# Second mixer: two more gates ahead of the transposes of branch B's keys, and fill products between the latents' steps

## The chip, the cores and the metric

The kernel runs on one core of a Trainium2 chip. The metric is the device time of one execution in microseconds (us), lower is better. One core has a matrix engine (TensorE, PE in the rows, with its weight loads as PEld), a vector engine (VectorE, DVE), an activation engine (ScalarE, ACT), a general one (GpSimd, POOL), and a queue that issues the DMAs (SyncE, SP). They run side by side and wait for each other through semaphores.

## The reference

A backbone of two layers over 256 latent tokens and 256 context tokens, 1024 wide. Each layer: a SwiGLU half step, three token mixers on one normalised input, a gated merge with an output projection, and a second SwiGLU half step. The context is an un-noised prefix; only the latent stream is returned.

```python
D_MODEL = 1024; SEQ = 256; CTX_LEN = 256; DEPTH = 2; D_FF = 2816
A_HEADS = B_HEADS = C_HEADS = 8; A_KV_HEADS = B_KV_HEADS = 2; HEAD_DIM = 64
C_NOPE_DIM, C_ROPE_DIM, C_V_DIM, C_Q_RANK, C_KV_RANK = 64, 32, 64, 384, 256
...
def mla_keys_values(c_kv, k_rope, p, rope):
    kv = heads(rms_norm(c_kv, p["c_kv_lat_norm"]) @ p["c_w_ukv"], C_HEADS)
    k_nope, v = kv[..., :C_NOPE_DIM], kv[..., C_NOPE_DIM:]
    k_rope = jnp.broadcast_to(k_rope[:, :, None, :], k_nope.shape[:-1] + (C_ROPE_DIM,))
    k = rms_norm(jnp.concatenate([k_nope, k_rope], axis=-1), p["c_k_norm"])
    return rope_tail(k, C_ROPE_DIM, rope), v
```

In words: A is grouped-query attention over a window with a sink, B the same over everything with normalised, rotated queries and keys, C attends through low-rank latents for queries and for keys and values. Each branch's output is projected, multiplied by a sigmoid gate of the normalised input (1024 columns for each branch), and the three are summed and projected.

## The kernel before, in words

**Products.** Everything is float32, and each product is made of three matmuls of rounded operands, high by high, high by low and low by high (`mm3`, L101 to L103). `split` makes the two halves of an operand: ScalarE copies the high one (L108), VectorE subtracts it (L109).

**Weights.** They come in chunks. `fetch` issues the DMA of a chunk on SP's queue (L172) into one of two `raw` buffers (q4 buffers alternate with them from the end of the mixer on, see below) and its split into `whi` and `wlo`, of which there are eight each. Chunks are fetched two ahead of their use. A chunk's DMA waits until the buffer's last chunk has been split, and the splits stand in the queues of ScalarE and VectorE among everything else these engines do.

**Order.** PE runs its instructions in the order of the program. The other engines' queues are laid out by a scheduler, which decides what stands ahead of what there.

**The mixer** (`mixer`, L1012). PE does attention in steps, and each step leaves PE with something to wait for: the scores of 128 queries against 512 keys (S, L710), a softmax on VectorE, ScalarE (exponential, L727) and GpSimd (scaling by the reciprocal sum, `p`, L736), four transposes of the result (T, L754), a split of them into `pth` and `ptl`, and after every second step a weighted sum of the values (O, L762 and L763). The scores have two PSUM buffers, so S of a step needs the exponential of two steps before. T stands two or three steps behind its S. Branch A has 16 steps, B 16 and C 16 (S0 to S15, two for each head).

Between these, `fill` draws on a list of products that nothing in the attention waits for: gates (24 matmuls of 128x256 each in the second mixer), branch B's queries (`w_bq`), the merges of finished branches (`w_br`), and the latents that branch C needs (`w_cq`, `w_ckv`). A generator runs through them in one order; `FILLS[l]` says how many us of it are drawn where in mixer `l`:

- `keys` and `start`: before and after the transposes of branch A's keys; `q`: ahead of the first scores of A; `a` and `b`: in each step of A and B
- `latent`: between the steps of `latent_heads` (L861: transposes of the normalised latents, L867); `ups`: before the products with `w_uq` and `w_ukv` that make C's queries and keys; `c0`: before C's attention; `c`: in each step of C
- at the end `fill(1e3)` draws all that is left

Inside the generator (L1073 to L1100) stand also the steps that prepare branch B: `prep_k` normalises and rotates B's keys (VectorE and GpSimd, L618 to L630; the last of it are the two multiplications by the gain, L630), and `k_heads` transposes them on PE (L670, four transposes, one for each 128 tokens, from the buffers `vh`, `vh`, `vh` and `th`).

At the end of the mixer `begin` (L186) copies a value of the last head's keys into `start`; from then on every second chunk goes to a q4 buffer, whose DMA waits for a copy from `start` on GpSimd (L154). The q4 buffers, three of them, hold C's keys until then. Then comes the merge of branch C (eight times 12 matmuls), which needs the whole output of C.

The second mixer does only the latent tokens (`last`), so its gates have 256 columns.

Of the kernel before, what the change touches and what calls it, by code (L numbers as in the profile page):

```python
# [14 lines left out]
KD = 8  # L15
# [12 lines left out]

FILLS = (
    dict(a=2.0, b=1.7, keys=0.0, start=9.0, q=3.0, latent=2.0, ups=5.0, c0=9.0, c=2.5),  # L30
    dict(a=2.0, b=1.8, keys=3.0, start=10.0, q=3.0, latent=0.0, ups=2.0, c0=0.0, c=1.3),
)
ADA_LOOK = 3
DEPTH_AB, DEPTH_C = 3, (2, 3)
# [24 lines left out]
class Kernel:  # L59
# [952 lines left out]
    def mixer(self, l, last, after):  # L1012
# [52 lines left out]
        def fill():  # L1065
            def gates(ds):
                for d in ds:
                    m.append(self.T(f"x{d}", [128, NT]))
                    yield from self.gate_tanh(l, 0, d, whole, m[d][:, whole])

            yield from gates(range(1))
            self.prep_k(g3, 1)
            yield from gates(range(1, 4))  # L1073
            self.K[1] = self.k_heads(g3, 1)
            self.rope_tables64((G_BQ,))
            bq.extend(self.raw4(512))
            yield from self.tok_product(l, "w_bq", 512, 2, bq, qtts, "d")
            left = list(qtts)
            for i, us in enumerate(gates(range(4, KD))):
                if left and i % 3 == 0:  # L1080
                    tt = left.pop(0)
                    self.prep_heads(bq[tt].rearrange("p (h d) -> p h d", h=8), G_BQ, tt, 8, self.rq[1][:, tt])
                yield us
            early = []
            if last:

                early += [v[:, HALF[1]] for v in m]
                for d in range(KD):
                    yield from self.gate_tanh(l, 1, d, whole, early[d])
            yield from self.merge(l, 0, y[0], m, whole, lambda: self.at > na)  # L1090
            c = self.T("m0", [128, 4, 384])
            cq.extend(c[:, tt] for tt in range(4))
            yield from self.tok_product(l, "w_cq", 384, 2, cq, qtts, "d")
            self.latent_norm(l, cq, 384, G_CQL, qtts)
            have.append(True)
            c = self.T("m1", [128, 4, 288])
            ckv.extend(c[:, tt] for tt in range(4))
            yield from self.tok_product(l, "w_ckv", 288, 3, ckv, (0, 1, 2, 3), "d")
            self.latent_norm(l, ckv, 256, G_CKVL, range(4))
            have.append(True)  # L1100
            yield from self.merge(l, 1, y[1], m, whole, lambda: ready, early)
            for i in (3, 4):
                c = self.T(f"m{i}", [128, 4, NT])
                ths.extend(c[:, j] for j in range(4))
            for d in range(KD):
                yield from self.gate_tanh(l, 2, d, whole, ths[d][:, whole])

        us = FILLS[l]
        fill = self.filler(fill())
        self.K = [None, None]  # L1110
        fill(us["keys"])
        self.K[0] = self.k_heads(g3, 0)
        fill(us["start"] - us["keys"])
        self.attention(steps, preps, lambda: fill(us["a"] if self.at < na else us["b"]), depth, lambda: fill(us["q"]))
        t3 = [self.T("q4", [128, 2, NT], F32R, bufs=Q4) for _ in range(3)]
# [11 lines left out]
        q = self.T("m6", [128, 4, 8, 96])  # L1127
# [32 lines left out]
        for d in range(0, KD, 2):  # L1160
            c = self.T(("pth", "ptl")[d // 2 % 2], [128, 2, NT], bufs=2)
# [4 lines left out]
        for v, tag, n, bufs in ((out[0], "m0" if last else "m5", 4, 1), (out[1], "m6", 6, 1), (out[1], "q4", 2, Q4)):  # L1166
            c = self.T(tag, [128, n, NT], F32R, bufs=bufs)
# [214 lines left out]
```

## Time and profile before

| | |
|---|---|
| Time, three runs | 2151.74, 2152.40 and 2154.44 us, median 2152.4 |
| The profiled execution | 2153.58 us, its span 2151.8 us |
| PE busy | 2097.2 us, 97% of the span |
| Chain of waits: PE, DVE | 90%, 5% |
| Granted TensorE clock, mean | 0.993 |
| Second mixer | about 1640 to 1926 us of the span |

The span runs from the first to the last instruction. The granted clock is a share of 2.4 GHz: 1.00 means that level, 0.50 means 1.2 GHz, and values between are means over a stretch with both. In a row of the timeline stand the start, the duration, engine, line, operation, output and inputs by the program's names, shape, how many such instructions the row takes together, and in brackets the idle time of the engine ahead of it and what ended it. Matmuls are pipelined: their durations overlap, and the pitch is read from the distance of two starts.

### The profile page before, as it was taken

To read this page: it belongs to the slowest core of one execution; us is meant where nothing else is said; L and a number is where in the kernel's file an instruction comes from. 1 tells how busy PE (TensorE), PEld (TensorE's weight loads), DVE (VectorE), ACT (ScalarE), POOL (GpSimd) and SP (SyncE) were. 2 spreads that over 40 slices of the span, in tenths; PEclk is the share of its full clock that TensorE was granted. 3 is DMA by queue.
4 is the path that set the end of the run, shared out by engine and by line. 5 is a ranking of instruction groups with operands and counts; after the bars stand their busy time and mean duration, and the time that the engine had idled before them with its cause. 6 is when DMAs were issued, how large, how long until landed. Compare 5 with 4: busy or idle time off the path is not lost.

```text
span 2151.8 us, 33450 instructions
## 1 busy us (share of the span) xinstructions
PE 2097.2 (97%) x11832; PEld 1829.3 (85%) x11832; DVE 1526.0 (71%) x3121; ACT 1008.5 (47%) x2026; POOL 445.1 (21%) x854
## 2 busy tenths in 40 slices
PE   6999999999999999999999999999999799999999
PEld 3888888888898888988888898888888798899999
DVE  5587777779888766658665666856568888986665
ACT  4323233567675664432323343232336676665554
POOL 3121110444234220202010031201105412511000
PEclk9999999999999999999999999999999899999999
DMA  8565555321113224256444326555543332345663
GB/s 297 194 203 176 175 174 167 98 79 53 45 49 104 68 64 143 79 182 199 149 153 140 107 82 204 191 173 181 175 145 110 109 99 76 104 142 177 188 187 120
DMA packets 95527, 299.17 MB, mean 139 GB/s; under 512 B 10880, under 2 KB 15616, under 8 KB 94976
## 3 DMA queue, kind: packets, MB, share of 16 engines
q1 hardware_dynamic: 95360, 297.04, 43.0%
q8 instruction: 93, 1.52, 0.3%
q14 instruction: 74, 0.61, 0.1%
HBM read 292.80 MB, written 4.19 MB: 138 GB/s over the span
## 4 chain that ended last, share of the span: by engine, by line
PE 90%; DVE 5%; ACT 1%; POOL 1%; DMA 1%; issue 1%; SPq 0%; POOLq 0%; ACTq 0%; DVEq 0%
PE pd L101 13%; PE pd L102 13%; PE pd L103 13%; PE ps L101 7%; PE ps L103 7%; PE ps L102 7%; PE pv L101 7%; PE pv L103 7%; PE pv L102 7%; PE ps L710 3%; PE pt L754 2%; PE pv L763 1%; DVE wlo L109 1%; PE pv L762 1%; POOL w L408 1%
## 5 line engine op out<-in xcount | busy, mean ns | idle before, releaser
L108 ACT ACTIVATE whi<-raw 128x512 fp32r<-128x512 f32 (+2 forms) x521 | 314.8, 611 | 466.9 <-PE pd L102 141.2
L109 DVE TENSOR_TENSOR wlo<-raw,whi 128x512 fp32r<-128x512 f32 (+2 forms) x521 | 349.9, 677 | 163.5 <-ACT whi L108 159.7
L108 ACT ACTIVATE whi<-q 128x512 fp32r<-128x512 f32 (+1 forms) x299 | 184.3, 620 | 380.2 <-PE pd L102 102.3
L101 PE MATMUL pd<-hh,whi 128*128 128x512 f32 (+1 forms) x864 | 304.5, 352 | 3.1 <-ACT hh L409 1.9
L102 PE MATMUL pd<-hl,whi 128*128 128x512 f32 (+1 forms) x864 | 302.1, 350 | 1.2 <-DVE hl L410 1.1
L103 PE MATMUL pd<-hh,wlo 128*128 128x512 f32 (+1 forms) x864 | 301.5, 349 | 0.0
L109 DVE TENSOR_TENSOR wlo<-q,whi 128x512 fp32r<-128x512 f32 (+1 forms) x299 | 200.4, 674 | 121.2 <-ACT whi L108 119.6
L154 POOL COPY q<-start 1x1 f32<-1x1 f32 x151 | 54.5, 362 | 656.2 <-DVE wlo L109 472.6
L101 PEld LDWEIGHTS pd<-hh,whi 128*128 128x128 f32 x864 | 163.8, 190 | 26.0 <-ACT hh L409 2.3
L102 PEld LDWEIGHTS pd<-hl,whi 128*128 128x128 f32 x864 | 163.9, 190 | 22.0 <-DVE hl L410 1.9
L101 PE MATMUL pv<-hh,whi 128*128 128x512 f32 (+1 forms) x512 | 182.3, 356 | 0.0
L102 PE MATMUL pv<-hl,whi 128*128 128x512 f32 (+1 forms) x512 | 182.2, 356 | 0.0
L103 PE MATMUL pv<-hh,wlo 128*128 128x512 f32 (+1 forms) x512 | 182.2, 356 | 0.0
L103 PEld LDWEIGHTS pd<-hh,wlo 128*128 128x128 f32 x864 | 163.8, 190 | 21.0
L102 PE MATMUL pd<-m,whi 128*128 128x512 f32 (+1 forms) x530 | 177.7, 335 | 0.5 <-DVE m L774 0.4
L101 PE MATMUL pd<-m,whi 128*128 128x256 f32 (+1 forms) x522 | 175.6, 336 | 0.5 <-DVE x L991 0.5
L103 PE MATMUL pd<-m,wlo 128*128 128x256 f32 (+1 forms) x522 | 174.6, 335 | 0.0
L101 PE MATMUL ps<-hh,whi 128*128 128x512 f32 (+1 forms) x480 | 169.0, 352 | 1.1 <-DVE w L495 1.1
L103 PE MATMUL ps<-hh,wlo 128*128 128x512 f32 (+1 forms) x480 | 168.1, 350 | 0.0
L102 PE MATMUL ps<-hl,whi 128*128 128x512 f32 (+1 forms) x480 | 168.1, 350 | 0.0
L736 POOL TENSOR_SCALAR p<-p,rd 128x512 f32<-128x512 f32 (+1 forms) x144 | 98.0, 685 | 295.9 <-DVE rd L734 183.0
L267 DVE SCALAR_TENSOR_TENSOR m<-pth,go,m 128x1024 f32<-128x1024 f32 x112 | 140.0, 1279 | 21.3 <-POOL go L265 12.9
(323 smaller groups left out, 4894.7 us busy)
## 6 DMA issues: line engine op xcount, KB each, us to landing
q<-ffn_in SPq DMA_DIRECT2D x86, 512.0 KB, 3.6
raw<-ffn_in SPq DMA_DIRECT2D x86, 512.0 KB, 3.9
pth<-ada_t SPq DMA_DIRECT2D x64, 512.0 KB, 4.3
ptl<-ada_t SPq DMA_DIRECT2D x64, 512.0 KB, 4.3
raw<-w_gate SPq DMA_DIRECT2D x48, 512.0 KB, 3.4
q<-ffn_out SPq DMA_DIRECT2D x32, 448.0 KB, 3.3
raw<-ffn_out SPq DMA_DIRECT2D x32, 448.0 KB, 3.3
raw<-w_br SPq DMA_DIRECT2D x41, 256.0 KB, 2.6
```

Source lines behind the costliest of these rows:

```text
L101: mm(out, lhsT=ah, rhs=bh, start=first, stop=False)
L102: mm(out, lhsT=ah, rhs=bl, start=False, stop=False)
L103: mm(out, lhsT=al, rhs=bh, start=False, stop=last)
L108: self.nc.scalar.activation(out=hi, in_=src, func=AF.Copy)
L109: self.nc.vector.tensor_tensor(out=lo, in0=src, in1=hi.bitcast(F32), op=ALU.subtract)
L154: nc.gpsimd.tensor_copy(out=raw[0:1, 0:1], in_=self.start)
L267: nc.vector.scalar_tensor_tensor(out=junk[:, i], in0=raw, scalar=go, in1=cb[:, i], op0=ALU.mult, op1=ALU.mult, accum_out=o[:, j, i:i + 1])
L408: nc.gpsimd.tensor_scalar(out=h, in0=v, scalar1=g, scalar2=s, op0=ALU.mult, op1=ALU.add)
L710: nc.tensor.matmul(s, lhsT=a, rhs=b[:, ks], start=(i == 0), stop=(i == len(ops) - 1 and not mask))
L736: nc.gpsimd.tensor_scalar(out=p[:, i], in0=p[:, i], scalar1=rd[:, i:i + 1], scalar2=1.0, op0=ALU.mult, op1=ALU.mult)
L754: nc.tensor.transpose(tr[:, kt, i * 128:(i + 1) * 128], p[qts][:, i, kt * 128:(kt + 1) * 128], self.ident)
L762: nc.tensor.matmul(o, lhsT=v, rhs=PT[0][:, kt], start=(kt == 0), stop=False)
```

## The change

Four numbers of `FILLS[1]` go up: `q` from 3 to 5, `latent` from 0 to 1, `ups` from 2 to 3, `c0` from 0 to 3. And in the second mixer (`last`), gates 1 to 5 instead of 1 to 3 stand in the list of fill products ahead of the transposes of branch B's keys; the other gates come behind branch B's queries, as before. No product is added or removed. The first mixer's order stays as it is.

```diff
@@ FILLS
-    dict(a=2.0, b=1.8, keys=3.0, start=10.0, q=3.0, latent=0.0, ups=2.0, c0=0.0, c=1.3),
+    dict(a=2.0, b=1.8, keys=3.0, start=10.0, q=5.0, latent=1.0, ups=3.0, c0=3.0, c=1.3),
@@ mixer, fill
             yield from gates(range(1))
             self.prep_k(g3, 1)
-            yield from gates(range(1, 4))
+
+            n = 6 if last else 4
+            yield from gates(range(1, n))
             self.K[1] = self.k_heads(g3, 1)
...
-            for i, us in enumerate(gates(range(4, KD))):
+            for i, us in enumerate(gates(range(n, KD))):
```

VectorE's queue, at the preparation of B's keys in the second mixer. The names: `vh_15911`, `vh_15912` and `th_15913` are the second, third and fourth block of B's keys, `wlo_...<-raw_...` is the split of a weight chunk. Before:

```order
L109 TENSOR_TENSOR q_3532_16528<-pt_16523,q_3532_16528 64x2x256
L627 TENSOR_TENSOR vh_15911<-vh_15911,r_16371 128x128
L637 TENSOR_REDUCE ss_16381<-w_16379 128x2
L637 TENSOR_REDUCE ss_16391<-w_16389 128x2
L623 TENSOR_TENSOR vh_15911<-vh_15911,tab_3489_16348 128x128
L118 TENSOR_SCALAR v_16383<-ss_16381 128x2
L118 TENSOR_SCALAR v_16393<-ss_16391 128x2
L624 TENSOR_TENSOR vh_15911<-vh_15911,w_16374 128x128
L627 TENSOR_TENSOR vh_15912<-vh_15912,r_16385 128x128
L630 TENSOR_TENSOR vh_15912<-vh_15912,gt_13727 128x128
L627 TENSOR_TENSOR th_15913<-th_15913,r_16395 128x128
L630 TENSOR_TENSOR th_15913<-th_15913,gt_13727 128x128
```

With the change, in the same place (`raw_16629` and `raw_16639` are the third and fourth chunk of `w_bq`; five rows, those for the sums of squares and the second block's rotation, are left out):

```order
L109 TENSOR_TENSOR q_3532_16528<-pt_16523,q_3532_16528 64x2x256
L627 TENSOR_TENSOR vh_15911<-vh_15911,r_16371 128x128
L109 TENSOR_TENSOR wlo_16632<-raw_16629,whi_16631 128x512
L623 TENSOR_TENSOR vh_15911<-vh_15911,tab_3489_16348 128x128
L109 TENSOR_TENSOR wlo_16636<-raw_16629,whi_16635 128x512
...
L109 TENSOR_TENSOR wlo_16642<-raw_16639,whi_16641 128x512
L109 TENSOR_TENSOR wlo_16646<-raw_16639,whi_16645 128x512
L627 TENSOR_TENSOR vh_15912<-vh_15912,r_16385 128x128
L627 TENSOR_TENSOR th_15913<-th_15913,r_16395 128x128
L630 TENSOR_TENSOR vh_15912<-vh_15912,gt_13727 128x128
L630 TENSOR_TENSOR th_15913<-th_15913,gt_13727 128x128
```

The splits of two more chunks now stand between the second block's first multiplication and the last two blocks. On PE the two gates, 48 matmuls, stand between the transposes of branch A's first queries (L687) and these of B's keys (L670).

PE's queue, at the end of branch C's attention, the last transposes and sums: T of S14, T of S15 and the O of head 7 before (`p_19665`, `p_19711`), fill products `pd_19756` and `pd_19817` between them:

```order
L754 MATMUL pt_19774<-ident,p_19665 128x128 x4
L762 MATMUL pv_19781<-pth_19698,vh_19455 128x256
...
L101 MATMUL pd_19756<-hh_15725,whi_19577 128x256
...
L754 MATMUL pt_19806<-ident,p_19711 128x128 x4
L101 MATMUL pd_19756<-hh_15725,whi_19581 128x256
...
L762 MATMUL pv_19833<-pth_19772,th_19566 128x256
...
L101 MATMUL pd_19817<-hh_15725,whi_19681 128x256
```

And with the change, from S14 on (`p_19736`, `p_19769` and `p_19791` are those of S13, S14 and S15; `pd_19883` is the first product of the merge of branch C):

```order
L710 MATMUL ps_19765<-q_4331_19710,hl_15726 128x512
L754 MATMUL pt_19780<-ident,p_19697 128x128 x4
L710 MATMUL ps_19787<-q_4331_19710,hl_15726 128x512
L762 MATMUL pv_19800<-pth_19723,vh_19508 128x256
...
L754 MATMUL pt_19813<-ident,p_19736 128x128 x4
L754 MATMUL pt_19822<-ident,p_19769 128x128 x4
L762 MATMUL pv_19829<-pth_19778,vh_19612 128x256
...
L754 MATMUL pt_19842<-ident,p_19791 128x128 x4
L762 MATMUL pv_19849<-pth_19820,th_19706 128x256
...
L101 MATMUL pd_19883<-m_4176_19064,whi_19481 128x256
```

Before, 99 fill matmuls of 128x256 stand on PE between S12 and the first matmul of C's merge, with the change none. 75 more stand between the steps of the latents for the keys and behind them, up to the products with `w_uq`'s second half, and 27 between these and the transposes ahead of C's first scores.

ScalarE's queue at the same place. Before, the exponentials of S14 and S15 (`p_19665`, `p_19711`) and the first split of a chunk in a q4 buffer (`q_4386_19907`):

```order
L727 ACTIVATE p_19665,den_19669<-ps_19661,nm_19666,rq_3380_15909 128x512
L772 ACTIVATE m_4138_18882<-pv_19720 64x256
L108 ACTIVATE whi_19886<-raw_19884 128x512
L727 ACTIVATE p_19711,den_19715<-ps_19707,nm_19712,rq_3380_15909 128x512
L108 ACTIVATE pth_19698<-pt_19745 128x4x128
L108 ACTIVATE whi_19910<-q_4386_19907 128x512
```

With the change (`p_19736`, `p_19769` and `p_19791` are the exponentials of S13, S14 and S15):

```order
L108 ACTIVATE whi_19910<-q_4386_19907 128x512
L108 ACTIVATE whi_19933<-raw_19931 128x512
L727 ACTIVATE p_19736,den_19740<-ps_19732,nm_19737,rq_3380_15909 128x512
L108 ACTIVATE pth_19778<-pt_19780 128x4x128
L108 ACTIVATE whi_19957<-q_4394_19954 128x512
L108 ACTIVATE whi_19980<-raw_19978 128x512
L727 ACTIVATE p_19769,den_19773<-ps_19765,nm_19770,rq_3380_15909 128x512
L772 ACTIVATE m_4176_19064<-pv_19800 64x256
L108 ACTIVATE whi_20004<-q_4402_20001 128x512
L108 ACTIVATE pth_19778<-pt_19813 128x4x128
L727 ACTIVATE p_19791,den_19795<-ps_19787,nm_19792,rq_3380_15909 128x512
```

Each of these three exponentials now has a split of a q4 chunk ahead of it; before, the last exponential stood ahead of the first such split. On GpSimd the copies that release the three q4 chunks stand together behind `p` of S12 and ahead of `p` of S13; the third takes the buffer of head 7's keys, which S14 and S15 read.

## Rows read from the trace of the kernel before

**Rows 1.** The page: busy time of each engine, chain that ended last.

```profile
PE 2097.2 (97%) x11832; PEld 1829.3 (85%) x11832; DVE 1526.0 (71%) x3121; ACT 1008.5 (47%) x2026; POOL 445.1 (21%) x854
...
PE 90%; DVE 5%; ACT 1%; POOL 1%; DMA 1%; issue 1%; SPq 0%; POOLq 0%; ACTq 0%; DVEq 0%
```

**Rows 2.** Windows over the second mixer: busy us, then PE's clock, DMA share, GB/s.

```profile
1650.00:1700.00 50.00, 41.61 (x237) 36.20 (x236) 40.73 (x88) 30.29 (x65) 22.58 (x27) 0.90 0.43 136
1700.00:1750.00 50.00, 47.60 (x370) 46.25 (x369) 44.40 (x105) 36.79 (x88) 15.60 (x16) 0.97 0.32 101
1750.00:1800.00 50.00, 48.60 (x355) 46.31 (x354) 41.66 (x104) 34.78 (x81) 12.70 (x17) 1.00 0.31 88
1800.00:1850.00 50.00, 44.73 (x271) 40.48 (x270) 42.23 (x111) 31.36 (x79) 19.91 (x34) 0.93 0.30 89
1850.00:1900.00 50.00, 47.78 (x342) 44.46 (x342) 47.31 (x117) 37.94 (x86) 20.89 (x26) 0.97 0.30 95
```

**Rows 3.** PE's timeline at the transposes of B's keys.

```profile
1671.35 0.60 PE L687 MATMUL pt<-ident,m 128*128 128x128 f32 x4
...
1679.72 0.48 PE L670 MATMUL pt<-ident,vh 128*128 128x128 f32 x1 [4.28 <-DVE vh L624]
...
1681.59 0.48 PE L670 MATMUL pt<-ident,th 128*128 128x128 f32 x1 [0.19 <-DVE th L630]
```

**Rows 4.** Timelines of SP, ACT and DVE there.

```profile
1674.63 3.01 SPq L172 DMA_DIRECT2D raw<-w_gate  x2
...
1675.32 1.15 ACT L108 ACTIVATE whi<-raw 128x512 fp32r<-128x512 f32 x2 [1.57 <-DMA raw<-w_bq]
...
1681.24 0.29 DVE L630 TENSOR_TENSOR th<-th,gt 128x128 f32<-128x128 f32 x1
```

**Rows 5.** The page's table of DMA issues: size, median us to landing.

```profile
raw<-w_gate SPq DMA_DIRECT2D x48, 512.0 KB, 3.4
...
q<-w_br SPq DMA_DIRECT2D x7, 256.0 KB, 2.7
```

**Rows 6.** PE's waits further on, from its timeline.

```profile
1702.71 1.11 PE L754 MATMUL pt<-ident,p 128*128 128x128 f32 x4 [2.40 <-POOL p L736]
...
1815.81 0.39 PE L763 MATMUL pv<-ptl,m 128*128 128x256 f32 x1 [0.57 <-DVE ptl L109]
...
1830.37 0.39 PE L101 MATMUL pd<-m,whi 128*128 128x256 f32 x1 [0.50 <-DVE x L991]
...
1847.11 0.61 PE L845 MATMUL pt<-ident,m 128*96 128x128 f32 x4 [1.38 <-DVE m L930]
```

**Rows 7.** Windows behind three of these waits, columns as in rows 2.

```profile
1682.00:1686.00 4.00, 4.00 (x12) 3.14 (x11) 1.40 (x3) 2.43 (x5) 0.00 (x0) 0.55 0.00 0
...
1702.00:1706.00 4.00, 3.29 (x14) 3.09 (x15) 4.00 (x9) 1.65 (x4) 4.00 (x4) 0.58 0.31 111
...
1853.00:1856.00 3.00, 3.00 (x15) 2.90 (x14) 3.00 (x8) 1.15 (x2) 1.61 (x2) 0.50 0.43 142
```

**Rows 8.** Timelines at the end of branch C's attention.

```profile
1893.16 0.28 PE L101 MATMUL pd<-hh,whi 128*128 128x256 f32 x1
...
1894.60 0.60 PE L845 MATMUL pt<-ident,m 128*96 128x128 f32 x4
...
1912.39 0.28 PE L763 MATMUL pv<-ptl,th 128*128 128x256 f32 x1
...
1896.33 0.69 POOL L736 TENSOR_SCALAR p<-p,rd 128x512 f32<-128x512 f32 x1 [2.49 <-DVE rd L734]
...
1897.20 0.29 POOL L154 COPY q<-start 1x1 f32<-1x1 f32 x2
...
1906.13 0.70 POOL L736 TENSOR_SCALAR p<-p,rd 128x512 f32<-128x512 f32 x1 [1.31 <-DVE rd L734]
...
1897.40 0.80 SPq L172 DMA_DIRECT2D q<-w_br  x2
...
1904.56 0.76 ACT L727 ACTIVATE p<-ps,nm,rq 128x512 f32<-128x512 f32 x1
```

## The prediction

> **What bounds the kernel now.** I read the page first: PE is busy 97% of the span, and it holds 90% of the chain that ended last [rows 1]. So the time is PE's work at its clock plus PE's idle time, and since the change neither adds nor removes a product, all it can do is move idle time and time at the lower clock. Then windows of 50 us over the second mixer [rows 2]: the reader is to see where PE falls short of 50. There are 8.4 us missing in 1650 to 1700, 2.4, 1.4, 5.3 and 2.2 in the four that follow, and the clock is below 1.00 in four of the five. Then PE's timeline for what ended each wait [rows 3, 6], the short windows behind the waits for the clock [rows 7], and last a place where PE does *not* wait now, the end of branch C's attention [rows 8], because the change takes away what fills it.
>
> **The fill products' price.** Twelve matmuls of 128x256 stand between 1893.16 and 1894.60 [rows 8], 0.12 us each; a gate of 24 is 2.9 us.
>
> **The keys' transposes.** PE is done with the first queries at 1671.95 and begins the last key transpose at 1681.59 [rows 3]. Two gates put PE there 5.8 us later, and if the keys were as early as before, 5.8 would be saved. But the order of VectorE's queue puts the splits of two more chunks ahead of the last two key blocks, and splits wait for their DMA: the split at 1675.32 waited 1.57 for its chunk [rows 4]. The chunk that stands in the third place of `w_bq` takes the DMA slot that begins at 1674.63; the fourth that which follows, 1677.3 (the row's 3.01 holds two issues of 0.33 each, its last ends at 1677.64) [rows 4]. A chunk of 512 KB lands 3.4 us after its issue by the median [rows 5]; here, where chunks follow one another closely, I take 3.8, so 1681.1. Its two splits take 1.15 on ScalarE and VectorE follows 0.7 behind, then four multiplications of some 0.3 [rows 4]: last key at about 1684.3 instead of 1681.5. So 2.9 of the 5.8 are saved. Bounds: 0, if the fourth chunk is a further 2.9 late; 5.8, if the keys lose nothing. The clock is at half for 3.3 us behind this wait (0.55 in 1682 to 1686 [rows 7]) and will be again, since a wait of some 6 us remains: no term.
>
> **Start of the attention.** The second stall there is T of an early step, 2.40 us for `p` on GpSimd [rows 6], which stands behind the rotation of B's queries on that engine; the clock is 0.58 over the 4 us behind it, worth 1.7 [rows 7]. With the change the queries' product comes later and `p` of the first three steps stands ahead of the rotation, so this stall goes; but the rotation then stands ahead of the fourth `p`. I take 2.7 of the 4.1 as saved, bounds 0 and 4.1.
>
> **Boundary of A and B, end of B.** One more step without fill at the boundary: the window has 1.4 idle now [rows 2], over two such steps; a third costs 0.7 (0 to 1.7). At the end of B the last two sums stand bare behind their split into `pth` and `ptl`, about 0.6 each on ScalarE and VectorE, where one wait of 0.57 stands now [rows 6]: about 1.2 for each sum, less the 0.57, and the transposes of the latents behind them are no earlier; with the lower clock 2.4 (1 to 3.5).
>
> **The latents and C's start.** Fill between the steps for the keys' latents takes away the 0.50 at 1830.37 [rows 6]: 0.5 saved. The 27 matmuls of `c0` (3.2 us) cover the 1.38 at 1847.11 [rows 6] and give VectorE time ahead of C's first scores; the clock at 0.50 in 1853 to 1856 costs 1.5 [rows 7]. I take 3.0 as saved for all; bounds 1.4 (the first wait alone) and 5.1 (that, the clock, and all of the 2.2 idle of 1850 to 1900 [rows 2]).
>
> **The end of C.** Here 99 fill matmuls, 11.9 us, leave PE. If PE had nothing to wait for, the merge would begin 11.9 us sooner after S12, and the loss would be nothing. Now S12 ends at 1893.16 and the merge begins at 1914.3 (last O at 1912.39 [rows 8], then 15 fills of 0.12): 21.1 us. With the change the chain from S12's end, by the same rows, is: `p` of S12 done at 3.9 (1896.33 plus 0.69); copy from `start` and issue of the q4 chunk at 4.2 (1897.40); landing 2.7 later [rows 5], 6.9; two splits on ScalarE of 0.6, 8.1; only then the exponential of S13, which stands behind them in ScalarE's queue, 0.76, so 8.9 [rows 4, 8]. S15 needs the PSUM buffer of S13: 9.6. The third q4 chunk takes the buffer of the keys that S15 reads: issue at 10.0, landing 12.7, split and one more split ahead of the last exponential, 13.9. From that exponential's start (1904.56) to the end of its `p` (1906.13 plus 0.70) it is 2.3 [rows 8]: 16.2. T, `pth`, `ptl` and eight matmuls of O: 18.9. So the merge begins 2.2 us sooner after S12 for 11.9 us of work that was moved out: 9.7 lost. PE idles for about half of that stretch, and after such a stretch the clock is at half for some 3.3 us [rows 7], 1.6 more: 11.3. Bounds: below, the same chain without the loads ahead of the exponentials. S15 then ends at about 5, its `p` 3.9 later (as S12's), O at 11.6: 7.3 less, and 4.0 lost, 2.4 if the clock holds. Above, all 11.9 and the clock: 13.5.
>
> The Trainium skill (the page TensorE: Matmul & The Clock Gate, section on the array's architectural detail) says that ScalarE and VectorE take their queues strictly in order. This trace agrees as far as it goes: the split that waited 1.57 for its DMA [rows 4] held what stood behind it. By that rule the exponentials wait for the loads and the tail loses 11.3; if something could pass a waiting split it would lose 4.0, and the sum would be 7.3 lower.
>
> **Sum.** -2.9 -2.7 +0.7 +2.4 -0.5 -3.0 +11.3 = +5.3 us. The profiled execution took 2153.6, 1.2 above the median of 2152.4; on the median it is 2157.7.
>
> **Rivals.** *The loads are there in time.* The price of the tail hangs on one thing: whether the q4 chunks have landed when the exponential of S13 could start, some 3 us after S12. They are issued at 4.2, which speaks against it; for it speaks that the whole tail is then less than 12 us of PE's work. The point that decides is an issue before S12 ends. Then the tail loses 4.0 and the sum is -2.0, 2150.4; with the bounds of the front terms (5.8 for the keys, 4.1 at the start) -6.3, 2146.1. *The two gates cover all of the keys' wait.* It is so if the fourth chunk lands within 1 us or the scheduler's order costs VectorE nothing: 2.9 less, 2154.8. Against it speaks the wait of 1.57 for a chunk [rows 4]. *The change doesn't do what it says.* The two chunks' splits delay the keys by as much as the gates take, and the stall on `p` moves to the next step: neither 2.9 nor 2.7 is saved, 2163.3. For it: both are orders that the scheduler laid out anew around the same DMAs.
>
> **How the numbers follow.** Forecast 0.43, loads in time 0.34, keys fully covered 0.11, no gain in front 0.12. A measurement of this kernel can tell about 0.2%, 4.3 us: faster is below 2148.1, slower above 2156.7. The forecast, 2157.7 with front terms that move by 3 either way, is slower for 0.29 and the same for 0.14. Loads in time is faster for 0.20 (with much of the front terms' upper bounds) and the same for 0.14. Keys fully covered splits 0.02, 0.05 and 0.04. The last is slower. Faster 0.22, same 0.33, slower 0.45. The range 2147 to 2164 leaves out about one in ten on each side: the best of the cases where the loads are in time, and the tail at its upper bound together with no gain in front. The forecast alone is 2154 to 2161.
>
> **What the profile after would show.** Keys: PE waits about 6 us in front of the second to fourth transposes instead of 8.4, for VectorE. Start: no wait of T for `p` above 1.3. End of B: waits of 1 us ahead of the last two sums. C's start: no wait for L930. End of C: PE idle for about 9 us between S13 and the last O, S15 released by an exponential that waited for a split of a q4 chunk, the merge's first matmuls at the half clock. I am wrong if PE runs through the tail in 12 us, or if the waits in front go below 2 us.

## The result, and the profile after

| | before | with the change |
|---|---|---|
| Time, median of five runs | 2152.4 us | 2165.93 us (2164.44 to 2168.79) |
| Ratio, with its 95% interval | | 1.0063 (1.0052 to 1.0074) |
| The profiled execution, its span | 2153.58, 2151.8 us | 2165.52, 2163.7 us |
| PE busy | 2097.2 us | 2102.1 us |
| Granted clock, mean | 0.993 | 0.992 |

The change makes the kernel 13.5 us slower. Slower was forecast, but by 5.3 us, and 2165.93 lies above the range. The span grew by 11.9 us: PE's busy time by 4.9, its idle time by 7.0.

The windows answer to [rows 2]; the columns are the same, and a fifth one takes in the end of branch C.

```profile
1650.00:1700.00 50.00, 44.17 (x266) 39.20 (x265) 41.37 (x91) 30.39 (x66) 19.81 (x24) 0.93 0.45 145
1700.00:1750.00 50.00, 47.11 (x369) 45.18 (x368) 46.22 (x107) 39.33 (x94) 20.85 (x21) 1.00 0.32 99
1750.00:1800.00 50.00, 48.57 (x350) 45.97 (x348) 42.16 (x105) 32.60 (x76) 12.06 (x16) 1.00 0.28 82
1800.00:1850.00 50.00, 43.58 (x278) 40.26 (x277) 37.44 (x89) 28.51 (x72) 17.94 (x31) 0.90 0.36 101
1850.00:1900.00 50.00, 46.45 (x320) 42.80 (x319) 43.78 (x115) 34.71 (x79) 20.07 (x22) 0.97 0.28 89
1900.00:1950.00 50.00, 41.96 (x304) 38.94 (x303) 38.53 (x89) 29.04 (x62) 6.78 (x16) 0.93 0.38 128
```

PE was idle for 5.8 us of the first window where it had been idle for 8.4: a gain of 2.6. The windows from 1800 on are idle for 1.1, 1.3 and, at the end, 7.0 us more than before (8.0 for 1.0 in the last). But windows at fixed times hold different work in the two kernels. So I measured between the same instructions, and took off the fill that stands between them in one kernel and not in the other, by the count of the order and 0.12 us for each 128x256 matmul. The landmarks are the first queries' transposes (L687), the T of three steps, the first transposes of the latents (L867) and the first of C's queries and keys (L845; before at 1847.11 [rows 6]). Before, the T of B's last step, the latents' transposes, the T of C's S0 and of S9:

```profile
1813.56 0.60 PE L754 MATMUL pt<-ident,p 128*128 128x128 f32 x4
1816.75 0.60 PE L867 MATMUL pt<-ident,m 128*128 128x128 f32 x4
1861.71 0.49 PE L754 MATMUL pt<-ident,p 128*128 128x128 f32 x3
1892.02 0.49 PE L754 MATMUL pt<-ident,p 128*128 128x128 f32 x3
```

And with the change L687, the last transpose of B's keys, the third and fifth T of branch A, the same landmarks of B and C, and the merge's first matmul:

```profile
1672.57 0.60 PE L687 MATMUL pt<-ident,m 128*128 128x128 f32 x4
1685.60 0.42 PE L670 MATMUL pt<-ident,th 128*128 128x128 f32 x1
...
1703.47 0.60 PE L754 MATMUL pt<-ident,p 128*128 128x128 f32 x4
1714.71 0.63 PE L754 MATMUL pt<-ident,p 128*128 128x128 f32 x4 [1.19 <-DVE den L732]
...
1812.40 0.60 PE L754 MATMUL pt<-ident,p 128*128 128x128 f32 x4
1818.88 0.41 PE L867 MATMUL pt<-ident,m 128*128 128x128 f32 x1
1860.16 0.60 PE L845 MATMUL pt<-ident,m 128*96 128x128 f32 x4
1874.62 0.63 PE L754 MATMUL pt<-ident,p 128*128 128x128 f32 x2
1904.80 0.60 PE L754 MATMUL pt<-ident,p 128*128 128x128 f32 x4
...
1925.66 0.41 PE L101 MATMUL pd<-m,whi 128*128 128x256 f32 x1
```

| Stretch | before | after | fill more (+) or less (-) | lost by the change | forecast |
|---|---|---|---|---|---|
| L687 to B's last T | 142.2 | 139.8 | +0.8 | -3.2 | -4.9 |
| B's last T to L867 (the end of B) | 3.2 | 6.5 | -0.8 | +4.1 | +2.4 |
| L867 to L845 (the latents) | 30.4 | 41.3 | +12.2 | -1.3 | -0.5 |
| L845 to C's first T (C's start) | 14.6 | 14.5 | 0 | -0.1 | -3.0 |
| C's first T to that of S9 | 30.3 | 30.2 | -0.3 | +0.2 | 0 |
| T of S9 to the merge | 22.3 | 20.9 | -11.8 | +10.4 | +9.7 |
| the merge's start at the half clock | | | | +0.5 | +1.6 |

It adds up to 10.6 of the 11.9; 1.2 lie ahead of L687 (1672.57 for 1671.35 [rows 3]), where both programs are the same, and belong to the execution.

**The end of branch C** went as worked out. The rows answer to [rows 8]: S12's last matmul on PE; GpSimd's `p` of S12, the copies, the third copy, and `p` of S15; SP's issues; VectorE's last step (`nm`, the negated maximum) ahead of S13's exponential; ScalarE's splits and exponentials of S13 and S15; then PE's S15, T of S14 and last O.

```profile
1905.70 0.40 PE L710 MATMUL ps<-q,hl 96*128 96x512 f32 x1
...
1909.03 0.69 POOL L736 TENSOR_SCALAR p<-p,rd 128x512 f32<-128x512 f32 x1 [0.47 <-DVE rd L734]
1909.90 0.29 POOL L154 COPY q<-start 1x1 f32<-1x1 f32 x2
1914.61 0.65 POOL L154 COPY q<-start 1x1 f32<-1x1 f32 x1 [4.42 <-DVE nm L722]
1920.73 0.69 POOL L736 TENSOR_SCALAR p<-p,rd 128x512 f32<-128x512 f32 x1 [1.98 <-DVE rd L734]
...
1910.10 5.51 SPq L172 DMA_DIRECT2D q<-w_br  x3
...
1912.01 0.16 DVE L722 TENSOR_TENSOR nm<-nm,rq 128x1 f32<-128x1 f32 x1
...
1912.82 0.63 ACT L108 ACTIVATE whi<-q 128x512 fp32r<-128x512 f32 x1 [1.06 <-DMA q<-w_br]
1913.87 0.76 ACT L727 ACTIVATE p<-ps,nm,rq 128x512 f32<-128x512 f32 x1
1917.95 0.63 ACT L108 ACTIVATE whi<-q 128x512 fp32r<-128x512 f32 x1 [0.54 <-DMA q<-w_br]
1918.96 0.77 ACT L727 ACTIVATE p<-ps,nm,rq 128x512 f32<-128x512 f32 x1
...
1914.78 0.73 PE L710 MATMUL ps<-q,hh 96*128 96x512 f32 x2 [2.48 <-ACT p L727]
1918.80 0.66 PE L754 MATMUL pt<-ident,p 128*128 128x128 f32 x4 [1.66 <-POOL p L736]
1923.28 0.58 PE L762 MATMUL pv<-pth,th 128*128 128x256 f32 x1 [0.69 <-ACT pth L108]
```

Counted from S12's end (1905.94, as the next matmul's pitch would have it): `p` of S12 done at 3.8 (forecast 3.9), the loads issued at 4.2 (4.2), the split at 6.9 (6.9), S13's exponential at 7.9 (8.1), S15 over at 9.7 (9.6), the last exponential begun at 13.0 (13.9), its `p` done at 15.5 (16.2), the merge at 19.7 (18.9). The reader is to see that the exponential of S13 begins at 1913.87, though VectorE had its `nm` ready at 1912.17: two splits stand ahead of it (the second, of 0.61, is not shown), and the first of them waited 1.06 for its DMA.

**The start of branch C** did not. ScalarE's rows, the `nm` of S0 on VectorE, PE's S2, and PE's S2 before:

```profile
1864.16 1.16 ACT L108 ACTIVATE whi<-raw 128x512 fp32r<-128x512 f32 x2 [0.69 <-DMA raw<-w_gate]
1867.05 0.63 ACT L108 ACTIVATE whi<-raw 128x512 fp32r<-128x512 f32 x1 [1.73 <-DMA raw<-w_gate]
1869.77 0.78 ACT L727 ACTIVATE p<-ps,nm,rq 128x512 f32<-128x512 f32 x1 [0.89 <-DVE nm L722]
...
1869.59 0.14 DVE L722 TENSOR_TENSOR nm<-nm,rq 128x1 f32<-128x1 f32 x1
...
1870.69 0.73 PE L710 MATMUL ps<-q,hh 96*128 96x512 f32 x2 [2.63 <-ACT p L727]
...
1858.81 0.73 PE L710 MATMUL ps<-q,hh 96*128 96x512 f32 x2 [0.70 <-ACT p L727]
```

The 1.38 for L930 [rows 6] is gone, as forecast, but S2 waits 2.63 for the exponential of S0, where it waited 0.70 before. Ahead of that exponential, ScalarE waited 0.69 and 1.73 for chunks of gate weights; but the last thing that it waited for is `nm` on VectorE, and VectorE had no gap ahead of it. A window of the changed kernel, the columns as in [rows 2]:

```profile
1860.00:1870.00 10.00, 7.74 (x57) 6.84 (x55) 10.00 (x26) 5.89 (x13) 7.25 (x5) 1.00 0.47 157
```

Six splits of gate weights (L109) took 4.1 us on VectorE between L845 and S2. From S0's scores to S2's it is 7.8 us in both kernels (1862.89 to 1870.69, before 1850.97 to 1858.81): before, the fill there ran in part at the half clock (0.50 in 1853 to 1856 [rows 7]); now it runs at the full clock and PE waits, and the clock falls behind S2 (0.57 in 1872 to 1876). So nothing was gained.

### The profile page after: what moved, and what is told of

It reads as the page before. It is cut to its first block, busy times and chain, and to the rows that moved or that the text cites. A ratio compares the mean times of both kernels' runs of the same rounds, so it can differ in the third digit from the quotient of the medians.

```text
span 2163.7 us, 33452 instructions
## 1 busy us (share of the span) xinstructions
PE 2102.1 (97%) x11832; PEld 1830.0 (85%) x11832; DVE 1527.3 (71%) x3121; ACT 1007.9 (47%) x2026; POOL 446.1 (21%) x854
## 4 chain that ended last, share of the span: by engine, by line
PE 85%; DVE 7%; DMA 3%; ACT 2%; issue 1%; POOL 1%; SPq 0%; ACTq 0%; POOLq 0%; DVEq 0%
PE pd L101 12%; PE pd L102 12%; PE pd L103 12%; PE ps L101 7%; PE pv L103 7%; PE pv L101 7%; PE ps L102 7%; PE pv L102 7%; PE ps L103 7%; PE ps L710 2%; DVE wlo L109 2%; PE pt L754 2%; POOL w L408 1%; DVE nm L717 1%; PE pv L763 1%
## 5 line engine op out<-in xcount | busy, mean ns | idle before, releaser
L109 DVE TENSOR_TENSOR wlo<-raw,whi 128x512 fp32r<-128x512 f32 (+2 forms) x521 | 350.7, 679 | 167.5 <-ACT whi L108 158.9
L109 DVE TENSOR_TENSOR wlo<-q,whi 128x512 fp32r<-128x512 f32 (+1 forms) x299 | 200.3, 674 | 119.0 <-ACT whi L108 116.4
```

The lines of the kernel that those rows point to most:

```text
L109: self.nc.vector.tensor_tensor(out=lo, in0=src, in1=hi.bitcast(F32), op=ALU.subtract)
```

## The experiments

Each ran five rounds against the kernel before on the same chip; a chip's median of that kernel was 2151.8 to 2153.9 us, so the ratios compare better than the times.

### The two halves of the change

Six gates ahead of the keys, and q=5, without the rest:

```diff
-    dict(a=2.0, b=1.8, keys=3.0, start=10.0, q=5.0, latent=1.0, ups=3.0, c0=3.0, c=1.3),
+    dict(a=2.0, b=1.8, keys=3.0, start=10.0, q=5.0, latent=0.0, ups=2.0, c0=0.0, c=1.3),
```

> One part alone: six gates ahead of the keys' transposes and q=5, with latent, ups and c0 as before the change, so that the fill products last through the end of branch C. Theory (the end of C takes the loss, the front saves a little): the front gain stays, some 2 to 3 us, 2149.5 to 2151. Rival (the new order in front costs as much as it saves, or the loss is made there): 2152.4 or more.

Measured: 2153.97 for 2151.83, ratio 1.0012 (1.0003 to 1.0020): slower by a little, as the rival had it. By the same landmarks this kernel was 3.7 us ahead at B's last T and 0.3 at C's first. The waits in between, PE's list of waits from 1805 to 1870 of this run (us in total, how many, the longest):

```profile
PE pv L763 <- DVE ptl L109: 2.5, 2, 1.9
PE pv L762 <- ACT pth L108: 1.9, 1, 1.9
PE pt L867 <- DVE q L109: 1.7, 1, 1.7
PE ps L710 <- DVE q L109: 1.6, 1, 1.6
PE ps L710 <- ACT p L727: 1.4, 1, 1.4
```

The larger lead leaves B's last sums bare (2.5 and 1.9 in total), and C's first scores wait 1.6 and 1.4. So the saving in front is real in this run and is given back before C begins, most of it from B's last T to the latents' transposes (4.1 lost).

The other half, with four gates and q=3:

```diff
-            n = 6 if last else 4
+            n = 4 if last else 4
...
+    q=3.0, latent=1.0, ups=3.0, c0=3.0
```

> The other part alone: latent=1, ups=3, c0=3 with four gates ahead of the keys and q=3. The end of branch C is bare from S13 on, with the exponentials of S14 and S15 behind splits of late chunks, but that of S13 ahead of them. Theory (bare end): slower than before by 7 to 12 us, 2159 to 2164. Rival (the loss needs both parts): within 2 us of 2152.4.

Measured: 2162.59, ratio 1.0048 (1.0035 to 1.0062). Here is the loss; the two halves, 1.0012 and 1.0048, come close to the 1.0063 of both.

The gates alone, with q as before:

```diff
-    q=5.0, latent=1.0, ups=3.0, c0=3.0
+    q=3.0, latent=0.0, ups=2.0, c0=0.0
```

> Six gates ahead of the keys' transposes and nothing else of the change (q stays 3, latent 0, ups 2, c0 0). The fill then ends each stage where it did before, so the last steps of branch B keep theirs. Theory (the front saves some 4 us, and in the run with q=5 the bare end of B gave it back): 2147 to 2149.5. Rival (the front saves nothing on the clock of the whole kernel): 2151 to 2154.

Measured: 2154.39 for 2153.09, ratio 1.0006 (0.9997 to 1.0015), so the theory failed: no gain. This kernel was 6.2 us ahead at the third T of A and 1.0 at the sixth; in between one T waits 2.87 for VectorE's `ptl`. The wait saved at the keys came back by the sixth T.

### The end of branch C

The release of the q4 buffers moved behind C's merge, in the changed kernel and in the one before:

```diff
-        self.begin(self.last_k[0:1, 0:1])
         fill(1e3)
...
         for _ in self.merge(l, 2, hl, m, whole, ths=ths, out=out):
             pass
+        self.begin(out[0][KD - 1][0:1, 0:1])
```

> The changed kernel with the release of the q4 buffers for weight chunks put behind branch C's merge, so that no split of such a chunk stands ahead of the last exponentials. Theory (the loads ahead of the exponentials stretch the bare end): the end is 7 us shorter, 2158 to 2160. Rival (the chain from scores to sum is as long without them): 2163 to 2167.

> Control: the kernel before with the same late release. Theory: the chunks for the output projection come later, but the merge's 96 matmuls lie ahead of them: 2151 to 2155. Rival (the late release itself costs much, so the run beside it tells little): over 2157.

Measured: 2157.87, ratio 1.0026 (1.0018 to 1.0035), and the control 2153.36, ratio 1.0007 (0.9998 to 1.0016). From 1.0063 to 1.0026 is 8 us, the theory's 7 and a little more. Rows of the changed kernel with the late release: S12's end, S15 on PE, the last exponential, its `p`, the merge.

```profile
1905.07 0.40 PE L710 MATMUL ps<-q,hl 96*128 96x512 f32 x1
1911.78 0.50 PE L710 MATMUL ps<-q,hh 96*128 96x512 f32 x1 [0.31 <-ACT p L727]
...
1914.85 0.77 ACT L727 ACTIVATE p<-ps,nm,rq 128x512 f32<-128x512 f32 x1
...
1916.10 0.70 POOL L736 TENSOR_SCALAR p<-p,rd 128x512 f32<-128x512 f32 x1 [1.17 <-DVE rd L734]
...
1920.06 0.28 PE L101 MATMUL pd<-m,whi 128*128 128x256 f32 x1
```

From S12's end to the merge it takes 14.8 us instead of 19.7, S15 waits 0.31 instead of 2.48, and the merge starts at the full clock. From T of S9 to the merge this run lost 5.5 us to the kernel before, the changed kernel 10.4. So the loads ahead of the exponentials were about half of what the bare end costs; the rest, 5.5 us by the landmarks, is the bare chain itself. That is 5 of the 8 us, and the merge's start at the full clock is 0.5 more; the rest isn't placed, for the execution shown was 3.0 earlier already at L687 (1669.59), ahead of every edit.

Less fill in each step of C, so that some is left for the last ones:

```diff
-    q=5.0, latent=1.0, ups=3.0, c0=3.0, c=1.3
+    q=5.0, latent=1.0, ups=3.0, c0=3.0, c=1.0
```

> The changed kernel with c=1.0 in place of 1.3, so that each step of branch C draws less fill and 1.1 us of it is left for every step to the last. Theory (the loss is the bare end): 8 to 10 us faster than the changed kernel, 2156 to 2158. Rival (thinner steps wait for their softmax all through branch C and the loss is only spread): 2162 to 2167.

Measured: 2162.26, ratio 1.0044 (1.0032 to 1.0057): 4 us better than the change, half of what I expected. Fill of 1.1 us stood between the steps up to S15's scores, 0.7 behind these, and none from T of S13 on, and the merge's start still ran at the half clock (0.50 in 1921 to 1924). With c thinner yet:

```diff
-    q=5.0, latent=1.0, ups=3.0, c0=3.0, c=1.3
+    q=5.0, latent=1.0, ups=3.0, c0=3.0, c=0.8
```

> The changed kernel with c=0.8, so that fill lasts to the end and about 4 us of it are left behind S15. Theory (the loss at the end is missing fill, there as well as between the last steps): faster than the run with c=1.0, 1.002 to 1.004 of before. Rival (with less fill in each step, the steps wait for their softmax all through C): 1.0045 or more.

Measured: 2159.99 for 2153.55, ratio 1.0030 (1.0018 to 1.0041). Fill behind the last steps does count: by the landmarks 2.3 us were lost from T of S9 to the merge, for 10.4. The thinner steps cost less than the rival said, but not nothing: 2.9 from C's first T to that of S9, for 0.2. The rest is ahead of C: 3.1 lost from B's last T to C's first, against 3.4 gained in front.

### The start of branch C

The kernel before with one number changed, c0=3 (the diff), and then latent=1 instead:

```diff
-    q=3.0, latent=0.0, ups=2.0, c0=0.0
+    q=3.0, latent=0.0, ups=2.0, c0=3.0
```

> The kernel before with c0=3 alone: 27 fill matmuls ahead of branch C's first scores, the end of C still filled. As predicted beforehand (they cover the waits at C's start): 3 us faster, 2149. Theory now (they only move the first scores behind more splits of weight chunks, whose loads are late): within 1.5 us of before, 2150.5 to 2153.5.

> The kernel before with latent=1 alone: fill between the steps of the latents, the end of C still filled. As predicted beforehand: 0.5 us faster. Theory now (the products drawn there wait for their own sums on VectorE, 1.3 us): 2152 to 2154. A change of over 3 us to either side would speak against both.

Measured: 2159.96 for 2153.09, ratio 1.0030 (1.0018 to 1.0041), and 2159.36, ratio 1.0030 (1.0019 to 1.0042). Both expectations failed, that of the prediction by 10 us with c0: either edit alone costs 6 to 7 us, though fill stands between most steps at the end of C. By the landmarks 2.2 and 3.1 were lost from B's last T to C's first, and 2.8 and 2.9 from T of S9 to the merge, where the last sums stand bare. For C's start I looked at ScalarE in the run with c0=3; its rows ahead of the first exponential of C:

```profile
1855.21 1.15 ACT L108 ACTIVATE whi<-raw 128x512 fp32r<-128x512 f32 x2 [2.96 <-DMA raw<-w_gate]
1859.26 0.63 ACT L108 ACTIVATE whi<-raw 128x512 fp32r<-128x512 f32 x1 [2.90 <-DMA raw<-w_gate]
1859.80 0.76 ACT L727 ACTIVATE p<-ps,nm,rq 128x512 f32<-128x512 f32 x1
```

It waited 5.9 us for loads, with C's first exponential behind them, and S2 waited 2.42 for that. But VectorE had no gap here either (9.00 of 9.00 us in 1850 to 1859) and was done with this exponential's `nm` only at 1859.42, so the late loads alone held it up by 0.4. To test loads and splits together I left them out: branch C's gates use the weights of the first, so seven loads of 512 KB and 14 splits go, and every matmul stays.

```diff
+            wg = self.chunk("w_gate", (l, 0, 2), 1024) if last else None
             for d in range(KD):
-                yield from self.gate_tanh(l, 2, d, whole, ths[d][:, whole])
+                g = self.P("d")
+                yield from self.col_fill(wg, KD, self.h_rhs(), g, whole)
+                nc.scalar.activation(out=ths[d][:, whole], in_=g[:, whole], func=AF.Tanh, scale=0.5)
```

(in the second mixer only). In the changed kernel:

> The changed kernel with seven of branch C's eight gates computed from the first gate's weights: seven loads of 512 KB and their 14 splits are left out (so those gates are not the reference's), every matmul stays. These are the loads that stand in front of the first exponentials of branch C. Theory (the waits at C's start are splits of chunks that have not landed): the wait of 2.6 us of S2 goes and with it the clock drop, 3 to 5 us faster than the changed kernel, 2161 to 2163. Rival (VectorE's own work on keys and queries is what is late there): within 1.5 us of it, 2164.5 to 2167.

With the late release as well:

> The same, with the release of the q4 buffers put behind branch C's merge as well, so that at the end of C no split stands ahead of the exponentials either. Leaves out the same seven loads. Theory (both losses are loads ahead of exponentials, and they add): 8 us below the run without gate loads, 2153 to 2155.5. Rival (the bare end costs the same whatever stands ahead of it): 2158 or more.

In the kernel before:

> Control: the kernel before with the same seven loads left out. Its gates of branch C are drawn later, under steps that hide them. Theory: little to gain, 2150 to 2152.5. Rival (the loads cost before as well): under 2149.

Measured: 1.0037 (1.0024 to 1.0049), 1.0020 (1.0011 to 1.0029) and 0.9994 (0.9985 to 1.0003). The changed kernel gains 5.6 us by it, the one before 1.3. S0, S1 and S2 in the changed kernel without these loads:

```profile
1862.42 0.63 PE L710 MATMUL ps<-q,hh 96*128 96x512 f32 x2
1864.54 0.63 PE L710 MATMUL ps<-q,hh 96*128 96x512 f32 x2
1866.66 0.63 PE L710 MATMUL ps<-q,hh 96*128 96x512 f32 x2
```

S2 waits for nothing, and from L845 to C's first T it takes 9.8 us (1859.69 to 1869.44) where the changed kernel took 14.5. With both kinds of loads out of the way 4.3 us are left, not the at most 1.6 of the expectation. By the landmarks of that run they are at the end of C: 6.8 lost from T of S9 to the merge, and 4.2 gained ahead of it.

The same in the kernels with c0=3 alone and latent=1 alone:

> The kernel before with c0=3 alone, and seven of branch C's eight gates computed from the first gate's weights (those gates are not the reference's; the seven loads and their splits are left out). With the loads this edit cost 7 us, though the end of C kept its fill. Theory (most of it is loads ahead of the first exponentials; some 2 us are the fill missing behind S15): 1 to 3 us slower than before. Rival (the fill at C's start costs for another reason): 5 us or more slower.

> The same for latent=1 alone (seven loads left out). With the loads it cost 6 us. Theory: loads ahead of exponentials are 2 to 3 of it, fill missing behind the last steps 2 to 3, so 2 to 4 us slower than before. Rival (the sums that the merge's products wait for between the latents are all of it): 5 us or more slower.

Measured: 2153.69 for 2153.55, ratio 1.0001 (0.9992 to 1.0010), and 2155.09, ratio 1.0006 (0.9998 to 1.0015). Of 6 to 7 us, 0.1 and 1.5 stay, less than either theory allowed. Windows from 1860 to 1868 with c0=3, without the loads and with them, the columns as before:

```profile
1860.00:1868.00 8.00, 8.00 (x65) 7.74 (x65) 4.81 (x14) 4.74 (x12) 2.62 (x4) 1.00 0.00 0
```

```profile
1860.00:1868.00 8.00, 7.30 (x44) 6.92 (x44) 5.28 (x15) 5.09 (x11) 3.49 (x5) 0.79 0.32 120
```

PE full and at the full clock in the first, idle for 0.7 and at 0.79 in the second. From B's last T to C's first these two runs gained 0.6 and 1.2 where 2.2 and 3.1 had been lost; from T of S9 to the merge they still lost 1.8 and 4.5. So at C's start what comes with moved fill is the cause, its loads and their splits together, and not the place of the fill; at the end the missing fill still costs. No run takes out the loads and leaves the splits, so the two are not told apart.

### Loads that land sooner

Each chunk of `w_gate` and `w_bq` in two DMAs of 256 KB, nothing left out:

```diff
-            nc.sync.dma_start(out=raw[:, :n], in_=src)
+            if name in ("w_gate", "w_bq"):
+                nc.sync.dma_start(out=raw[:, :512], in_=src[:, :512])
+                nc.sync.dma_start(out=raw[:, 512:n], in_=src[:, 512:n])
+            else:
+                nc.sync.dma_start(out=raw[:, :n], in_=src)
```

> The kernel before with each chunk of w_gate and w_bq fetched as two DMAs of 256 KB, so that the first half can be split while the second is on its way. Theory (splits that wait for loads hold up what stands behind them): 1 to 3 us faster, 2149 to 2151.5. Rival (more issues on SP's queue, nothing sooner): 2152 or more.

> The changed kernel with each chunk of w_gate and w_bq fetched as two DMAs of 256 KB. Nothing is left out. Theory (late loads hold up the keys and the first exponentials of C): the first half lands sooner, 2 to 4 us faster than the changed kernel, 1.0045 to 1.0055 of before. Rival (what counts is when the second half lands): within 1 us of the changed kernel, about 1.006.

Measured: in the kernel before 0.9997 (0.9988 to 1.0006), no gain; in the changed one 1.0037 (1.0023 to 1.0050) for 1.0063, 5.6 us faster, more than expected. S2 waited 1.5 in it instead of 2.63, with all splits in place, so the landing of the loads is part of the matter; by the landmarks 1.8 of the gain lie between B's last T and C's first, 1.4 ahead of these and 0.8 at the end.

Last, the two versions of the front with these half loads, latents and C as before, first with q=5, then with q=3:

```diff
-    q=5.0, latent=1.0, ups=3.0, c0=3.0
+    q=3.0, latent=0.0, ups=2.0, c0=0.0
```

> Six gates ahead of the keys and q=5, the other numbers as before the change, with each chunk of w_gate and w_bq fetched in two DMAs. The front of this order saved 4 us up to the end of branch B and lost them ahead of C's first scores, behind gate loads. Theory (the halves land sooner, so part of the saving stays): 1 to 3 us faster than the kernel before. Rival (only the place of the wait changes): within 1.5 us of it.

> The same with q=3. Theory: the stalls that followed the saved wait in the run with whole chunks, in the first steps of branch A, shrink; 1 to 3 us faster than the kernel before. Rival: within 1.5 us of it.

Measured: with q=5 ratio 1.0018 (1.0009 to 1.0027), with q=3 2151.41 for 2153.61, ratio 0.9990 (0.9981 to 0.9999). With q=5 theory and rival both failed: it is 2.9 us slower. The last is the only version that beats the kernel before, by 2 us and just clear of noise. The two differ in q alone, and by the landmarks most of the difference is at the end of B: from B's last T to the latents' transposes q=5 lost 4.1 and q=3 gained 0.2.

## Why the prediction was wrong

Right: the sign, the mechanism and the size of the largest term. **The end of C** was put at +11.3 and lost 10.9, with each instant of the chain within 1 us of the forecast, and the late release showed that the loads ahead of the exponentials stretch it. In part the sizes cancel: the last `p` was done 0.7 sooner than forecast, and T and O behind it took 1.5 longer, at the half clock (0.50 in 1921.5 to 1925.6); PE was idle for 5.4 us between S13 and the last O, not for 9. By the strict order that the Trainium skill states for ScalarE (TensorE: Matmul & The Clock Gate, the array's architectural detail) S13's exponential had to wait for the split; it did. **The keys' transposes**, -2.9: from L687 to the last of them it took 13.0 us (1672.57 to 1685.60) instead of 10.2 [rows 3], with 5.8 of gates inside, so 3.0 were saved.

Wrong, first: **C's start**, put at -3.0 and measured at -0.1. The step that failed is that the 27 matmuls of `c0` "give VectorE time ahead of C's first scores". They did cover the 1.38. But a fill product is not PE's time alone: it draws its chunk, and the chunks that follow two ahead, and VectorE has to split them. It was busy for 10.00 of 10.00 us in 1860 to 1870 (before, for 11.00 of 11.00 in 1847 to 1858), and splits took 4.1 between L845 and S2; so it was given no time, and S2 waited 2.63. I had seen at the end of C and for the keys that splits come with the fill, and did not look for it here; I gave the term bounds of 1.4 to 5.1 *saved*. With seven loads and their splits left out the same stretch is 4.7 us shorter; then the term would have been -4.8. Edits c0 and latent alone cost 6 to 7 us, and without the loads and splits 0.1 and 1.5.

Second, smaller: **the end of B**, put at +2.4, lost 4.1: its last sum waited 1.93 for `pth` and 1.70 for `ptl` where I had taken 1.2 for each sum, and the clock was at 0.50 in 1818 to 1824. The latents gave 1.3 back, for a forecast of 0.5.

Third, **start of the attention**, put at -2.7 with "the rotation then stands ahead of the fourth `p`". Behind the keys 4.7 us were gained by the third T of A (1703.47) and 3.5 lost again by the fifth: PE waited 1.37 for `ptl`, 0.34 and 1.19, while GpSimd, with the rotation, was busy without a gap (8.00 of 8.00 us in 1704 to 1712). Net -1.2. The run with the gates alone, where the stall only moved five steps on, says the same: my rival that the stall moves was right for more than half of this term.

The rivals: that the loads would be there in time was wrong by the rows (issued at 4.2 after S12, as worked out). The upper end of the range, 2164, was made of the tail's upper bound and no gain in front; it could not hold that tail together with a dearer end of B and no saving at C's start. A reading was off, too: the 3.3 us at the half clock are 3.6 by the row that they are from (0.55 over 4 us), which moves no term by more than 0.2.

What stays open: whether the loads or the work of their splits cost more at C's start. Per us of fill, gates and merges bring the same bytes and splits (24 matmuls for 512 KB and two splits, 12 for 256 KB and one), so what makes gates there dearer isn't shown. The stretch from L845 to C's first T also moves from one execution to another: the run with the gates alone, which has the fill of the kernel before there, took 17.4 us for 14.6. And the median of the run with c0 alone is 3 us worse than its profiled execution shows by the landmarks (6.9 for 3.8); with latent alone the two agree (6.3 and 5.8).

## What to carry to other kernels

A fill product carries its loads and the splits of its weights with it: when fill is moved, read on the other engines' queues what now stands behind the splits, when their DMAs land, and whether the engine that splits has any idle time left. Fill taken from the end of a chain that nothing else covers can be lost at almost its full price: here 11.8 us moved out cost 10.4, and 5.5 where no load stood ahead of the exponentials. And a wait that is covered at one place reappeared here a few steps on, so a saving counts only at the next landmark behind which the order is the same.

## What was unexpected of the hardware

Fetching a 512 KB chunk as two DMAs of 256 KB moved the time by 5.6 us in the changed kernel and by nothing (0.9997) in the one before, though ScalarE waited for such chunks in both (12.5 and 7.4 us in the second mixer, 1660 to 1930). And kernels whose programs are the same up to there reached the second mixer's first queries anywhere between 1669.5 and 1673.2 us in the profiled executions, so spans of single executions can't tell 3 us apart here.
